# One stage for all value projections, and weights that are split again for each block, in a two-layer trunk kernel

## The chip, the cores and the metric

The kernel runs on one core of a Trainium2 chip. The metric is device time in microseconds of one launch. A core has TensorE (PE, matrix products and transposes), VectorE (DVE), ScalarE (ACT), GpSimd (POOL) and SyncE (SP), which here issues every DMA. Each engine works through a queue of its own in order, and semaphores order the engines against each other.

## The reference

x is 2048 rows of 1024 in fp32. Layer A is a gated mixer, layer B band attention with 16 heads of 64, where a chunk of 64 rows sees itself and the 8 chunks before it:

```
x = x + gmlp(rms_norm(x, g_a), ...)             # layer A
k, v = split(rms_norm(x, g_kv) @ w_kv)          # shared keys and values
q, z = split(rms_norm(x, g_b) @ w_qz)           # layer B
p = softmax(q / 8 @ k.T + rel_bias[clip(rel)])  # 64 rows against 576
x = x + ((p @ v) * silu(z)) @ w_out
out = rms_norm(x, g_f)
```

All weights are inputs, read in fp32. The keys' and values' gain g_kv and the layer's gain g_b multiply the rows of the weights, so both projections share one normalized x.

## The kernel before, in words

**Products.** Every operand of a product is split into a high part (rounded to fp32r by a cast on ACT) and a low part (what is left, a subtraction on DVE). One fp32 product is three matmuls, high x high, high x low and low x high (mm3, L115 to L118).

**Layer A** (0 to about 1347 us) leaves its result in DRAM as x1d, four blocks of 512 rows. Near its end three weights of pair 0 are scaled by POOL and stored (k_scale), and the sums of value weights that Strassen's scheme needs are stored as vwf, 7 phases x 2 halves of 128x1024.

**Layer B** goes over four time blocks t (512 rows each) and in each over 8 pairs p of heads. For a pair it projects Q, K and gate Z (24 matmuls of 128x512 each; one calls weights), then for 8 units u: score (scores, reduction with bias on DVE, exp on ACT, scaling on POOL), flip (five transposes on PE, cast on ACT, subtraction on DVE) and value (probabilities times V). ahead(t, p) is a generator that yields after each group of three matmuls; the loop at the end takes its steps between the units, so that projection of the next pair fills PE while softmax goes on.

**Values.** All values of a block come from one Strassen product (strassen, 7 phases x 2 tiles x 12 = 168 matmuls; order PHS = 1, 7, 2, 6, 5, 4, 3). For block 0 it runs during the first two scores; for block t+1 it is part of ahead(t, 7), together with normalizing x of the next block (b1: load of x1d, square on ACT, scaling on DVE, 32 transposes, copies). v_left makes the sums of x on POOL and splits them (split_s, L1106, L1107). Values go to DRAM (vhd) and are read back per pair. The **output projection** of a block is the same kind of product (o_all); its 56 steps of three matmuls are dealt out over the pairs of the next block by SHARE. Its left input, the gated output, goes through DRAM (ogd, stored at L1350), and its weights come from ows, whose sums o_sums makes during pairs 1 to 4 of t=0.

**Weights.** weights(t, p, c): at t=0 the raw weight is loaded (512 KB; pair 0 from wk0, already scaled), scaled by POOL (L163), split on ACT and DVE (L173, L174), and both halves are stored (L176, 1 MB); at t=1 to 3 the two halves are loaded ready made (kept_w, L182, 1 MB). Value weights are treated in the same way (vws). All of them live in tag T of the pool sh, 8 slots of 128x1024; tag raw has 4 slots.

**Order.** The framework lays out each engine's queue when the kernel is compiled and adds the semaphore waits; a DMA that waits on SP holds up all DMAs behind it.

Of the kernel before, what the change touches and what calls it, by code (L numbers as in the profile page):

```python
# [17 lines left out]
P = 128  # L18
# [15 lines left out]
def trunk_kernel(  # L34
# [25 lines left out]
    wk0 = [dram.tile([P, 1024], F32, name=f"wk0_{c}") for c in range(3)]  # L60
    wks = [
        [dram.tile([P, 2, 1024], F32, name=f"wks{p}_{c}") for c in range(3)] for p in range(NPAIR)
# [3 lines left out]
    }  # L66
    vws = {
        (ph, q): dram.tile([P, 2, 1024], F32, name=f"vws{ph}_{q}")
        for ph in range(1, 8) for q in range(2)
# [9 lines left out]
    vhd = [dram.tile([P, NPAIR, TB, 256], F32, name=f"vhd{t}") for t in range(NT)]  # L79
    ogd = [dram.tile([P, 2, NPAIR, 2, P], F32, name=f"ogd{t}") for t in range(NT)]  # L80
# [40 lines left out]
    xf = {}  # L121

# [4 lines left out]
    def b1(t, banks, junk):  # L127
# [4 lines left out]
        def norm(b):  # L132
            xt = sh.tile([P, D], F32, tag="raw", name=f"bx_b{t}_{b}", bufs=4)
            nc.sync.dma_start(xt[:], x1d[t][b * P : (b + 1) * P, :])
            r = sm.tile([P, 1], F32, tag="rr", name=f"rr_b{t}_{b}", bufs=4)
            nc.scalar.activation(
                junk(f"jk_b{t}_{b}"), xt[:], AF.Square, scale=1.0 / 32, accum_out=r[:]
            )
            root(r[:])
            nc.vector.tensor_scalar(xt[:], xt[:], r[:], None, op0=ALU.mult)  # L140
            xf[t, b] = xt

        def block(b):
            xt = xf[t, b]
            half = [banks(f"tr_b{t}_{b}_{h}") for h in range(2)]
            for k in range(KD):
                tpose(half[k // 4][:, k % 4, :], xt[:, k * P : (k + 1) * P], ident[:])
            x3 = xt[:].rearrange("p (k c) -> p k c", k=KD)
            for h in range(2):
                ks = slice(h * 4, h * 4 + 4)  # L150
                oh = th[:, ks, b * P : (b + 1) * P]
                ol = tl[:, ks, b * P : (b + 1) * P]
                nc.scalar.copy(oh, half[h])
                nc.scalar.copy(x3[:, ks, :], half[h])
                nc.vector.tensor_tensor(ol, half[h], oh.bitcast(F32), op=ALU.subtract)  # L155

        xT[t] = [(th[:, k, :], tl[:, k, :]) for k in range(KD)]
        return norm, block
# [6 lines left out]
    def gain_of(c):  # L165
        return (bg if c else kg)[:, :, :]

# [3 lines left out]
    def split_w(raw, name, keep):  # L171
        wh, wl = w_tile(f"wh_{name}"), w_tile(f"wl_{name}")
        nc.scalar.copy(wh[:], raw[:])  # L173
        nc.vector.tensor_tensor(wl[:], raw[:], wh[:].bitcast(F32), op=ALU.subtract)  # L174
        for i, w in enumerate((wh, wl)):
            nc.sync.dma_start(keep[:, i, :], w[:].bitcast(F32))  # L176
        return wh, wl

    def kept_w(keep, name):
        out = [w_tile(f"w{i}_{name}") for i in "hl"]  # L180
        for i, w in enumerate(out):
            nc.sync.dma_start(w[:].bitcast(F32), keep[:, i, :])  # L182
        return out
# [12 lines left out]
    def v_right(t):  # L196
        def right(ph):
            out = []
            for q in range(2):
                name = f"bv{t}_{ph}_{q}"  # L200
                if t:
                    out.append(kept_w(vws[ph, q], name))
                    continue
                raw = sh.tile([P, 1024], F32, tag="T", name=f"raw_{name}", bufs=8)
                nc.sync.dma_start(raw[:], vwf[ph, q][:])
                out.append(split_w(raw, name, vws[ph, q]))
            return out
        return right

    def o_right(t):  # L210
        def right(ph):
            return [kept_w(ows[ph, q], f"bo{t}_{ph}_{q}") for q in range(2)]
        return right

    with ExitStack() as actx:
# [698 lines left out]
        def k_scale(c):  # L914
            raw = sh.tile([P, 1024], F32, tag="raw", name=f"rk_{c}", bufs=4)
            nc.sync.dma_start(raw[:], w_kqz[0, :, c, :])
            scaled(raw, gain_of(c))
            later(2, lambda: paced(nc.sync.dma_start(wk0[c][:], raw[:])))

        for c in range(3):  # L920
            at(nin + 26 + 2 * c, lambda c=c: k_scale(c))

# [39 lines left out]
        blocks = []  # L962
        pt4x = ExitStack()

        def b_open():
            pt4 = pt4x.enter_context(tc.tile_pool(name="pt4", bufs=1, space=PSUM))
            blocks.append(b1(
                0, lambda n: pt4.tile([P, 4, P], F32, tag="t4", name=n, bufs=4)[:],
                lambda n: acc_tile(n)[:].bitcast(BF16),
            ))  # L970
            for b in range(2):
                blocks[0][0](b)

        def block0(b):
            blocks[0][1](b)
            if b < 2:
                blocks[0][0](b + 2)
# [17 lines left out]
        block0(3)  # L995
        pt4x.close()
        ptr.open(name="ptr", bufs=1, space=PSUM)
        px.close()


    with ExitStack() as bctx:
# [11 lines left out]

        sub, add = ALU.subtract, ALU.add
        tv, tg = nc.vector.tensor_tensor, nc.gpsimd.tensor_tensor
# [66 lines left out]

        PHS = (1, 7, 2, 6, 5, 4, 3)

        def strassen(name, right, left, evict):

            for ph in PHS:
                rt = right(ph)
                lt = left(ph)
                for jp in range(2):  # L1090
                    views = lt(jp)
                    ps = pmm.tile([P, 512], F32, tag="mm", name=f"{name}_{ph}_{jp}")
                    for k in range(4):
                        hi, lo = rt[k // 2]
                        c = slice((k % 2) * 512, (k % 2) * 512 + 512)
                        mm3(ps[:], *views[k], hi[:, c], lo[:, c], k == 0, k == 3)
                        if k < 3:
                            yield
                    evict(ph, jp, ps[:])
                    yield  # L1100

        def split_s(name, src):
            hi, lo = (
                sb.tile([P, 4, P], F32R, tag="S", name=f"S{i}{name}", bufs=6) for i in "hl"
            )
            nc.scalar.copy(hi[:], src)  # L1106
            tv(lo[:], src, hi[:].bitcast(F32), op=sub)  # L1107
            return [(hi[:, k, :], lo[:, k, :]) for k in range(4)]

        def v_left(t):  # L1110
            def quad(r, h):
                def of(jp):
                    c = slice((2 * jp + r) * P, (2 * jp + r + 1) * P)
                    return [(a[:, c], b[:, c]) for a, b in xT[t][4 * h : 4 * h + 4]]
                return of

            def raw(jp, r, h):
                return xf[t, 2 * jp + r][:, h * 512 : h * 512 + 512]

            def summed(ph, r, h):  # L1120
                def of(jp):
                    return split_s(
                        f"v{t}_{ph}_{jp}", raw(jp, r, h).rearrange("p (k c) -> p k c", k=4)
                    )
                return of

            def left(ph):
                if ph == 1:
                    for jp in range(2):
                        a11, a12, a21, a22 = (raw(jp, r, h) for r in range(2) for h in range(2))  # L1130
                        tg(a22, a21, a22, op=add)
                        tg(a21, a11, a21, op=sub)
                        tg(a11, a22, a11, op=sub)
                        tg(a12, a12, a11, op=sub)
                return {
                    1: quad(0, 0), 2: quad(0, 1), 4: quad(1, 1), 5: summed(5, 1, 1),
                    7: summed(7, 1, 0), 6: summed(6, 0, 0), 3: summed(3, 0, 1),
                }[ph]
            return left

        def v_evict(t):
            xa, ya = {}, {}

# [41 lines left out]
        def v_all(t):  # L1185
            yield from strassen(f"vp{t}", v_right(t), v_left(t), v_evict(t))
# [446 lines left out]
```

## Time and profile before

| | |
|---|---|
| median of 3 runs | 2928.61 us (2919.07 to 2932.9) |
| profiled execution | 2926.53 us |
| its span | 2924.7 us |
| granted TensorE clock, mean | 0.96 |
| DMA | 834.13 MB, mean 285 GB/s |
| HBM read / written | 619.20 / 201.85 MB |
| layer A | 0 to about 1347 us |
| layer B, t=0 | to about 1795 us (first score at 1369) |
| t=1, 2, 3 | to about 2161, 2521, 2816 us |
| rest of the output projection | to the end |

The span is the time from the first to the last instruction of the profiled execution. A line of the waits view names the engine that sat idle, the tile and line it was about to work on, the engine and line (or DMA) whose end released it, and then the total, the number of times and the longest. A line of the groups view gives the line, engine, operation, tiles, shapes and count, then busy time and mean duration of one, then idle time just before. Line numbers are those of the kernel before.

### The profile page before, as it was taken

Reading aid. Unit: us, or ns where it says so; the run is one execution under the profiler, and the core shown is the slowest. Engines: PE = TensorE matmul, PEld = TensorE weight load, DVE = VectorE, ACT = ScalarE, POOL = GpSimd, SP = SyncE. Lnnn points to the kernel's source line nnn. Section 1 sums busy time; section 2 is a strip of 40 time slices with the busy share of each in tenths; the row PEclk is TensorE's granted clock in tenths of the full one; section 3 lists DMA queues with packets and bytes.
Section 4 is the critical chain, followed back from the end, with each engine's and each line's share of the span. In section 5 each row is a group of like instructions: output and inputs, shape, how many; then the busy total and the mean of one; then the engine's idle time right before and its main releaser. Section 6 shows DMA issues by size and latency. Waiting matters only on the chain. (4 is left out here: it accounts for less than half of the span.)

```text
span 2924.7 us, 38938 instructions
## 1 busy us (share of the span) xinstructions
PE 2698.2 (92%) x13216; PEld 2237.6 (77%) x13216; DVE 1845.4 (63%) x3009; ACT 1246.8 (43%) x2274; POOL 888.1 (30%) x903
## 2 busy tenths in 40 slices
PE   9999999999999999998587689999899998999975
PEld 7788888888888888886365577788777887788854
DVE  5665776666776686774355465566765667566653
ACT  5332333434344343334244354455544555455532
POOL 4513153332514131232214343133322224122223
PEclk9999999999999999999787799999999999999987
DMA  8898989899888786885787788878888788986685
GB/s 304 319 326 329 377 323 326 319 344 328 316 287 306 269 337 208 287 315 196 261 287 247 247 298 288 284 244 274 284 297 293 240 277 281 301 258 215 219 291 208
DMA packets 302356, 834.13 MB, mean 285 GB/s; under 512 B 32592, under 2 KB 65360, under 8 KB 302160
## 3 DMA queue, kind: packets, MB, share of 16 engines
q1 hardware_dynamic: 302160, 831.67, 82.0%
q8 instruction: 105, 1.72, 0.2%
q14 instruction: 91, 0.75, 0.1%
HBM read 619.20 MB, written 201.85 MB: 281 GB/s over the span
## 5 line engine op out<-in xcount | busy, mean ns | idle before, releaser
L116 PE MATMUL P<-T,S 128*128 128x512 f32 x1248 | 495.2, 397 | 2.1 <-ACT S L265 2.1
L118 PE MATMUL P<-T,S 128*128 128x512 f32 x1248 | 489.4, 392 | 0.0
L117 PE MATMUL P<-T,S 128*128 128x512 f32 x1248 | 488.2, 391 | 0.6 <-DVE T L268 0.6
L1273 POOL TENSOR_SCALAR pr<-pr,sl 128x640 f32<-128x640 f32 (+4 forms) x256 | 199.2, 779 | 638.3 <-DVE sl L1272 593.9
L116 PE MATMUL pj<-hh_b,wh_b 128*128 128x512 f32 x768 | 317.9, 414 | 33.2 <-ACT wh_b L173 27.4
L118 PE MATMUL pj<-hh_b,wl_b 128*128 128x512 f32 x768 | 309.5, 403 | 12.9 <-DMA wl_b<-wks 12.5
L117 PE MATMUL pj<-hl_b,wh_b 128*128 128x512 f32 x768 | 308.7, 402 | 0.9 <-DVE hl_b L155 0.9
L1269 ACT ACTIVATE pr<-pr,nm 128x640 f32<-128x640 f32 (+4 forms) x256 | 195.3, 763 | 260.6 <-DVE nm L1262 254.9
L118 PEld LDWEIGHTS P<-T,S 128*128 128x128 f32 x1248 | 234.7, 188 | 50.2
L116 PEld LDWEIGHTS P<-T,S 128*128 128x128 f32 x1248 | 235.2, 188 | 47.0 <-ACT S L265 2.3
L117 PEld LDWEIGHTS P<-T,S 128*128 128x128 f32 x1248 | 235.2, 188 | 46.4 <-DVE T L268 1.0
L1297 DVE TENSOR_TENSOR pt<-tp,pt 128x640 fp32r<-128x640 f32 (+4 forms) x256 | 189.1, 739 | 115.4 <-ACT pt L1296 113.9
L1262 DVE CUSTOM_DVE_ANT_0 pr<-s,bias 128x640 f32<-128x640 f32 (+4 forms) x256 | 188.4, 736 | 44.7 <-PE s L1254 36.3
L116 PEld LDWEIGHTS pj<-hh_b,wh_b 128*128 128x128 f32 x768 | 149.8, 195 | 58.2 <-ACT wh_b L173 29.6
L118 PEld LDWEIGHTS pj<-hh_b,wl_b 128*128 128x128 f32 x768 | 148.6, 193 | 53.5 <-DMA wl_b<-wks 18.8
L1296 ACT CAST pt<-tp 128x640 fp32r<-128x640 f32 (+4 forms) x256 | 158.7, 620 | 64.6 <-PE tp L1293 60.8
L1293 PE MATMUL tp<-ident,pr 128*128 128x128 f32 x1120 | 168.2, 276 | 18.3 <-DVE pt L1297 13.9
L1293 PEld LDWEIGHTS tp<-ident,pr 128*128 128x128 f32 x1120 | 135.7, 141 | 57.0 <-issue 18.8
L117 PEld LDWEIGHTS pj<-hl_b,wh_b 128*128 128x128 f32 x768 | 149.3, 194 | 21.8 <-DVE hl_b L155 1.2
L1254 PE MATMUL s<-K,Qh 128*128 128x320 f32 (+1 forms) x448 | 118.3, 333 | 38.6 <-DVE nm L1262 29.2
L1321 PE MATMUL pv<-pt,V 128*128 128x256 f32 x960 | 144.9, 293 | 0.0
L1254 PEld LDWEIGHTS s<-K,Qh 128*128 128x128 f32 x448 | 84.3, 193 | 66.9 <-DVE nm L1262 39.0
(269 smaller groups left out, 5821.4 us busy)
## 6 DMA issues: line engine op xcount, KB each, us to landing
S<-hsd SPq DMA_DIRECT2D x288, 512.0 KB, 5.4
rw<-in_w_a SPq DMA_DIRECT2D x108, 512.0 KB, 6.2
A<-ytd SPq DMA_DIRECT2D x72, 512.0 KB, 5.9
wh_b<-wks SPq DMA_DIRECT2D x72, 512.0 KB, 6.2
wl_b<-wks SPq DMA_DIRECT2D x72, 512.0 KB, 6.5
hsd<-S SPq DMA_DIRECT2D x56, 512.0 KB, 4.4
V<-vhd SPq DMA_DIRECT2D x56, 512.0 KB, 4.8
wh_bo<-ows SPq DMA_DIRECT2D x56, 512.0 KB, 4.9
```

The source lines that it names most:

```text
L116: mm(ps, lh, rh, start=first, stop=False)
L117: mm(ps, lh, rl, start=False, stop=False)
L118: mm(ps, ll, rh, start=False, stop=last)
L1254: mm(ps[:, sg, :w], q[:, qb * P : (qb + 1) * P], kx[:, koff + sg * w : koff + (sg + 1) * w], start=i == 0, stop=i == 1,)
L1262: nc.vector.tensor_tensor_reduce(out=pr[:, c0:].rearrange("p (a b) -> p a b", a=nseg), in0=ps[:, :nseg, :w], in1=bias[:, c0:].rearrange("p ...
L1269: nc.scalar.activation(pr[:, c0:], pr[:, c0:], AF.Exp, scale=-1.0, bias=nm[:], accum_out=sl[:])
L1273: nc.gpsimd.tensor_scalar(pr[:, c0:], pr[:, c0:], sl[:], 1.0, op0=ALU.mult, op1=ALU.mult)
L1293: tpose(tp[:, b, :], pr[:, b * P : (b + 1) * P], ident[:])
L1296: nc.scalar.copy(oh, tp[:, b0:5, :])
L1297: nc.vector.tensor_tensor(pt[:, 1, b0 + qq : 5 + qq, cs], tp[:, b0:5, :], oh.bitcast(F32), op=ALU.subtract)
L1321: mm(po[:, 0, :], keys(i), pt[:, j, i, :], start=(t == 0 and j == 0 and i == blocks[0]), stop=(j == 1 and i == blocks[-1]),)
```

## The change

1. A **value stage** between the layers, in a pool of its own (vp). It loads each raw value weight once, splits it once and keeps the halves on chip: phases 1, 7, 5, 4, 3 in 20 tiles of the pool, phases 2 and 6 in the 8 slots of T. It makes the values of all four blocks in turn. While block t is worked on, x of block t+1 is loaded and normalized, and its 32 transposes stand at steps 20, 28, 36 and 44. For t >= 1 the transposed x goes to DRAM (xtd); pair 7 of block t-1 loads it again and splits it (reload). vws is gone, and b1 and v_all leave ahead.
2. **K, Q and gate weights**: at t=0 the raw weight is loaded, scaled, stored scaled (wk3, 0.5 MB) and split; at t >= 1 the raw weight is loaded (0.5 MB) and split again. Raw, high and low part all sit in T. k_scale leaves layer A.
3. **strassen looks one tile ahead**: after the second of a tile's four steps it asks for the next tile's weights and left input. o_left loads and sums earlier. For the last block the weights of phases 2 and 3 come raw and are split.
4. **Steps**: SHARE is (2, 7, 7, 7, 7, 7, 7, 12) in each block; the last block's output projection stands wholly behind the last pair; ahead(0, 0) begins during the first two scores.

The diff, cut to its core:

```diff
     def weights(t, p, c):
         name = f"b{t}_{p}_{c}"
+        raw = t_tile(f"raw_{name}")
+        w = w_tile(f"wh_{name}"), w_tile(f"wl_{name}")
         if t:
-            return kept_w(wks[p][c], name)
-        tag, n = ("raw", 4) if p else ("T", 8)
-        raw = sh.tile([P, 1024], F32, tag=tag, name=f"raw_{name}", bufs=n)
-        nc.sync.dma_start(raw[:], w_kqz[p, :, c, :] if p else wk0[c][:])
-        if p:
-            scaled(raw, gain_of(c))
-        return split_w(raw, name, wks[p][c])
+            nc.sync.dma_start(raw[:], wk3[p][c][:])
+        else:
+            nc.sync.dma_start(raw[:], w_kqz[p, :, c, :])
+            scaled(raw, (bg if c else kg)[:, :, :])
+            nc.sync.dma_start(wk3[p][c][:], raw[:])
+        split_in(raw, *w)
+        return w
...
+    def reload(t):
+        th, tl = x_tiles(t)
+        for b in range(TB):
+            xt = sh.tile([P, D], F32, tag="raw", name=f"xr_b{t}_{b}", bufs=4)
+            nc.sync.dma_start(xt[:], xtd[t][b][:])
...
+            nc.scalar.copy(oh, x3)
+            tv(tl[:, :, b * P : (b + 1) * P], x3, oh.bitcast(F32), op=sub)
...
     def strassen(name, right, left, evict):
...
+        ready(0)
+        for i, (ph, jp) in enumerate(todo):
...
                 mm3(ps[:], *vs[k], hi[:, c], lo[:, c], k == 0, k == 3)
+                if k == 1:
+                    ready(i + 1)
...
+    with ExitStack() as vctx:
+        vp = vctx.enter_context(tc.tile_pool(name="vp", bufs=1, reuse_waits="tile"))
+        vw = {
+            (ph, q): [vp.tile([P, 1024], F32R, name=f"vw{i}{ph}_{q}") for i in "hl"]
+            for ph in (1, 7, 5, 4, 3) for q in range(2)
+        }
+        def v_right(t):
+            def right(ph):
+                if t == 0:
+                    for q in range(2):
+                        if ph in (2, 6):
+                            vw[ph, q] = [w_tile(f"vw{i}{ph}_{q}") for i in "hl"]
+                        raw = vp.tile([P, 1024], F32, tag="st", name=f"st{ph}_{q}", bufs=2)
+                        nc.sync.dma_start(raw[:], vwf[ph, q][:])
+                        split_in(raw, *vw[ph, q])
+                return [vw[ph, q] for q in range(2)]
+            return right
...
+        for t in range(NT):
+            if t + 1 < NT:
+                for b in range(TB):
+                    norm(t + 1, b, v_junk)
+            for i, _ in enumerate(strassen(f"vp{t}", v_right(t), v_left(t), v_evict(t))):
+                if t + 1 < NT and i in (20, 28, 36, 44):
+                    block(t + 1, (i - 20) // 8)
...
-        SHARE = {1: (0, 9, 9, 9, 9, 10, 10, 0), 2: (0, 9, 9, 9, 9, 10, 10, 0)}
-        SHARE[3] = (0, 3, 4, 4, 4, 4, 4, 33)
+        SHARE = (2, 7, 7, 7, 7, 7, 7, 12)
...
-            elif t + 1 < NT:
-                norm, block = b1(t + 1, bank4, junk)
-                for b in range(TB):
-                    norm(b)
-                for b in range(TB):
-                    block(b)
-                    yield
-                yield from project(t + 1, 0)
-                yield from v_all(t + 1)
-                values(t + 1, 0)
-            if t:
-                yield from some(outs[t - 1], SHARE[t][p])
-            if t + 1 == NT and p + 1 == NPAIR:
-                yield from some(outs[t], 16)
+                if t:
+                    yield from some(outs[t - 1], SHARE[p])
+            else:
+                if t + 1 < NT:
+                    reload(t + 1)
+                if t:
+                    yield from some(outs[t - 1], 4)
+                if t + 1 < NT:
+                    yield from project(t + 1, 0)
+                    values(t + 1, 0)
+                if t:
+                    yield from some(outs[t - 1], 8)
```

More of the change, by code (lines that the diff above doesn't have):

```diff
@@ L79, in trunk_kernel @@
     vhd = [dram.tile([P, NPAIR, TB, 256], F32, name=f"vhd{t}") for t in range(NT)]
+    xtd = [[dram.tile([P, D], F32, name=f"xtd{t}_{b}") for b in range(TB)] for t in range(NT)]
     ogd = [dram.tile([P, 2, NPAIR, 2, P], F32, name=f"ogd{t}") for t in range(NT)]
@@ L121, in trunk_kernel @@
     xf = {}
+    banks = []
+    pt4x = ExitStack()
+    place = [lambda t, b: sh.tile([P, D], F32, tag="raw", name=f"bx_b{t}_{b}", bufs=4)]
+    sub, add = ALU.subtract, ALU.add
+    tv, tg = nc.vector.tensor_tensor, nc.gpsimd.tensor_tensor
     def root(r):
@@ L199, in right @@
             for q in range(2):
-                name = f"bv{t}_{ph}_{q}"
-                if t:
[L202 to L206, printed above, removed]
-            return out
-        return right
[L210 to L213, printed above, removed]
+                name = f"bo{t}_{ph}_{q}"
@@ L1102, in split_s @@
[L1102 to L1139, printed above, removed]
@@ L1533, in trunk_kernel @@
         run(gen)
-        gen = v_all(0)
+        values(0, 0)
+        first = ahead(0, 0)
         for u in range(2):
             score(0, 0, u)
-            take(gen, 8)
-        run(gen)
-        values(0, 0)
+            take(first, 4)
         before = None
```

319 lines of the change are left out of this document (168 added, 151 removed).

## The prediction

> **What bounds the kernel now.** I read the busy shares and the 40 slices of the page first, then stretches of the span by stage, then in each stage the waits of TensorE (PE), then single lines.
>
> ```profile
> span 2924.7 us, 38938 instructions
> PE 2698.2 (92%) x13216; PEld 2237.6 (77%) x13216; DVE 1845.4 (63%) x3009; ACT 1246.8 (43%) x2274; POOL 888.1 (30%) x903
> PE   9999999999999999998587689999899998999975
> PEclk9999999999999999999787799999999999999987
> ```
>
> PE is the bound in nearly every slice. The exceptions are slices 19 to 23 (1390 to 1750 us: layer B's block t=0) and the last two, and there the granted clock falls too. A gain can come from these holes or from work taken off PE. This change takes no matmul away, so only holes count.
>
> Next, stretches; columns are the window, its length, each engine's busy time (PE first, with its instructions), granted clock, DMA share, GB/s.
>
> ```profile
> 1060.00:1320.00 260.00, 260.00 (x1149) 215.29 (x1148) 184.74 (x215) 91.61 (x141) 67.68 (x42) 1.00 0.78 283
> 1347.00:1369.00 22.00, 15.81 (x61) 11.08 (x60) 11.89 (x12) 8.23 (x14) 6.68 (x10) 0.92 0.75 256
> 1369.00:1481.00 112.00, 69.13 (x189) 44.75 (x189) 41.77 (x74) 34.26 (x61) 20.37 (x21) 0.75 0.77 271
> 1532.00:1574.00 42.00, 32.52 (x134) 26.09 (x132) 23.93 (x52) 19.35 (x44) 19.93 (x24) 0.80 0.75 258
> 1574.00:1625.00 51.00, 34.65 (x137) 26.16 (x136) 23.44 (x55) 19.73 (x45) 17.19 (x23) 0.80 0.73 247
> 1625.00:1672.00 47.00, 33.58 (x129) 25.98 (x129) 22.63 (x51) 18.90 (x43) 17.47 (x23) 0.75 0.72 238
> 1672.00:1710.00 38.00, 31.31 (x138) 24.66 (x137) 19.11 (x46) 16.08 (x37) 14.07 (x19) 0.78 0.83 277
> 1710.00:1737.00 27.00, 25.50 (x137) 20.66 (x136) 19.73 (x48) 15.71 (x39) 11.65 (x20) 1.00 0.82 278
> 1737.00:1795.00 58.00, 50.94 (x252) 41.78 (x252) 31.74 (x72) 31.62 (x71) 21.54 (x30) 0.97 0.85 290
> 1795.00:2087.00 292.00, 275.02 (x1519) 233.25 (x1518) 184.07 (x372) 144.44 (x275) 77.11 (x105) 0.99 0.84 278
> 2087.00:2161.00 74.00, 63.65 (x325) 54.02 (x324) 50.67 (x93) 38.97 (x77) 27.82 (x29) 0.93 0.85 285
> 2446.00:2521.00 75.00, 65.31 (x332) 54.85 (x332) 51.52 (x93) 39.22 (x79) 28.07 (x30) 0.95 0.88 292
> 2816.00:2925.00 109.00, 60.91 (x220) 46.42 (x218) 41.18 (x71) 21.91 (x46) 30.27 (x27) 0.74 0.70 240
> ```
>
> The first row is a stretch of layer A with nothing but 128x512 matmuls at full clock: 260/1149 = 0.226 us each. For the others I count as **lost** the length less busy time times clock. The value projections of block 0 (1369:1481) lose 112 - 69.13x0.75 = 60 us. Pairs 2 to 5 of t=0 (the four rows 1532 to 1710) lose 16, 23, 22 and 14, together 75; pair 6 (1710:1737), with as many instructions, loses 1.5. Pair 7 of t=0, 1, 2, which carries the next block's value projections, loses 8.6, 14.8 and 13. The tail loses 109 - 60.91x0.74 = 64.
>
> **The change part by part.** One: the value projections of block 0. What holds them now:
>
> ```profile
> DVE wl_bv L174 <- ACT wh_bv L173: 48.0, 11, 8.6
> ACT wh_bv L173 <- DMA raw_bv<-vwf: 46.2, 7, 8.3
> PE vp L116 <- ACT wh_bv L173: 35.2, 12, 4.7
> SPq L176 <- ACT wh_bv L173: 35.0, 10, 5.9
> L173 ACT CAST wh_bv<-raw_bv x13: 1029/1044/1045, 1375.3 to 1475.2; 128x1024 fp32r<-128x1024 f32 x13
> L174 DVE TENSOR_TENSOR wl_bv<-raw_bv,wh_bv x13: 1220/1224/1993, 1376.6 to 1476.3; 128x1024 fp32r<-128x1024 f32 x13
> raw_bv<-vwf SPq DMA_DIRECT2D x13, 512.0 KB, 4.6
> ```
>
> It is a ring: PE waits for the split, the split for the raw load, and the load is queued on SP behind the store of the halves (L176), which waits for the split before. Thirteen casts from 1375.3 to 1475.2 make 99.9/12 = 8.3 us per half of a phase; 14 halves give the 112 us. The change drops both stores, gives raw data two buffers of their own (st), and holds the halves in place. A buffer then turns in load 4.6 + cast 1.04 + subtraction 1.22 + some 0.6 for issue and semaphores = 7.5 us, and two buffers serve one phase of two halves: 7 x 7.5 = 52 us. PE needs 168 x 0.226 = 38. From below it can't be under 38; from above the old pace gives 112. I take 52, the sum of the rows. The two scores that share the old window, some 4 us, move to later: **-56**. Ahead of it the transposes of block 1 and its four loads of x now stand in front of the first value matmul, and SP has those loads before the first raw weight: I take 11 us lost at the start, against 22 - 15.81x0.92 = 7 now: **+4** (0 to +15).
>
> Two: blocks 1 to 3 move from pair 7 of t=0, 1, 2 into the new stage. Each is 168 matmuls (38 us) and 32 transposes; the work goes along unchanged. In the new stage a block needs no weight traffic; ACT and DVE split halves of x and evict, as in pair 7 now, where DVE is busy 50.67 us of 74, so I take 4 us lost per block (0 to 10), mainly at the seams: +12. Where they leave, these waits go:
>
> ```profile
> PE pj L118 <- DMA wl_b<-wks: 11.4, 12, 2.3
> PE tr_b L147 <- DVE hl_b L155: 8.6, 4, 3.2
> PE pj L116 <- DMA wh_b<-wks: 5.5, 5, 2.0
> PE vp L117 <- DMA wl_bv<-vws: 4.7, 6, 1.3
> PE vp L116 <- DMA wh_bv<-vws: 3.6, 4, 1.4
> ```
>
> (PE alone, 1795 to 2521.) The rows tr_b and vp are pair 7's; they hold 17 of the 28 us that its t=1 and 2 lose. What comes in their place is four reloads of transposed x with a split (ACT, DVE) each, early in pair 7, and projection of the next block must wait for the last. I leave 5 us lost per pair 7, so -4, -10 and -8, about -23: **-11** together.
>
> Three: pairs 1 to 5 of t=0. Stores shrink from 1 MB of halves, after the split, to 0.5 MB of scaled raw data that waits for POOL alone; and in the order of instructions the gate weight's load now stands ahead of the store of K.
>
> ```profile
> PE pj L116 <- ACT wh_b L173: 23.7, 8, 4.7
> ACT wh_b L173 <- POOL raw_b L163: 22.5, 13, 3.3
> SPq L176 <- ACT wh_b L173: 37.5, 11, 6.3
> SPq L1062 <- DVE K L1058: 9.7, 4, 4.7
> raw_b<-in_w_kqz SPq DMA_DIRECT2D x17, 512.0 KB, 5.5
> L163 POOL TENSOR_TENSOR raw_b<-raw_b,bg x11: 1891/1896/2347, 1533.4 to 1721.0; 128x1024 f32<-128x1024 f32 x11
> ```
>
> (1495 to 1737.) The same ring, with POOL's 1.9 us in it. SP still has each next load behind a store, now behind POOL instead of the split (2.3 us shorter), and the gate weight skips the whole wait for K. Of three weights I give 2 us each for the split and 2 for K's store, 8 us per pair, over four pairs: **-32** of the 75 lost. From below it is 0, if the output-weight sums of these pairs (o_sums, unchanged) hold SP as before; at most -70, were they to run like pair 6.
>
> Four: at t=1 to 3 each of 72 weights comes as 0.5 MB raw and is split again. ACT gets 72 x 1.04 = 75 us more and DVE 72 x 1.22 = 88; both are under 70% busy there, DVE 184 of 292, so neither becomes the bound by sum. What counts is latency. Raw, high and low part take 3 of the 8 slots T, o's phase holds 4; so in the order of instructions the low part of two weights in three waits for the last matmul of the weight before, on DVE, with this weight's first two matmuls, five transposes and some value matmuls in PE's order between. DVE's queue behind it holds the flips' subtractions and the score reductions, for which PE waits next. A pair takes 292/7 = 42 us, 14 per weight, against load 5.5 + cast 1.04 + subtraction 1.22 = 8, so the load itself is hidden. What is exposed is bounded by pair 6 from below:
>
> ```profile
> L174 DVE TENSOR_TENSOR wl_b<-raw_b,wh_b 128x1024 fp32r<-128x1024 f32 x3 | 3.7, 1225 | 1.9 <-ACT wh_b L173 1.9
> L173 ACT CAST wh_b<-raw_b 128x1024 fp32r<-128x1024 f32 x3 | 3.1, 1043 | 0.7 <-POOL raw_b L163 0.7
> ```
>
> There three weights are split on chip and the pair loses 1.5 us, 0.5 each. From above all of cast, subtraction and 0.6 of semaphores shows, 2.9 each. I take pair 6's 0.5, for two of three weights: 48 x 0.5 = +24 (0 to +205). Half the weight bytes lets the loads land earlier: of the waits for wl_b and wh_b (17 us) I take 12 as gone. Net **+12**.
>
> A page speaks against this step. The Trainium skill, "SBUF — State Buffer", section "Who interferes with whom", says that a DVE instruction with two SBUF inputs contends with a GpSimd instruction that reads SBUF, and that the loser waits for the whole instruction. POOL is busy 77.11 of 292 us here; if a split in four met the 0.78 us of a POOL instruction (the next row), that would be 72 x 0.26 x 0.78 = 15 us of DVE time, and the sum would be 2825.
>
> ```profile
> L1273 POOL TENSOR_SCALAR pr<-pr,sl 128x640 f32<-128x640 f32 (+4 forms) x256 | 199.2, 779 | 638.3 <-DVE sl L1272 593.9
> ```
>
> The trace agrees in kind: of the 13 subtractions above the median is 1.22 us and the longest 1.99.
>
> Five: the tail.
>
> ```profile
> PE bo L116 <- ACT Sho L1106: 28.5, 3, 12.4
> ACT Sho L1106 <- DMA A<-ogd: 21.0, 2, 11.0
> ```
>
> (2815 to 2925.) Now a third of the last block's output projection stands in pair 7 and the rest stops three times for its left input, which makes a round trip through DRAM from the last pair's values. After the change all 56 steps stand behind pair 7: the last value product comes early, and phases 1 and 7 (11 us), which need only the first heads, cover the round trip; the look one tile ahead puts loads and splits a tile earlier. Then weights bound it: 2 MB per phase, at the 290 GB/s of the best row above 7 us for 5.4 us of matmuls, and 1 MB for phases 2 and 3, which come raw. I leave 5 of the 28.5 us of waits; the clock, 0.74 now, comes back to about 0.9, worth 60.91 x 0.2 = 12: **-35** (0 to -50). The even shares of the output projection in other pairs, and the key scaling that leaves layer A (three loads and stores under a full PE), I take at 0: PE is the bound there; if one of them uncovered a load, a wait of about 2 us like those above.
>
> **Sum:** +4 - 56 - 11 - 32 + 12 - 35 = -118. The profiled execution took 2926.5 us; the median of the three is 2928.6, 2 above. So **2810 us**, a saving of 4%.
>
> **Rivals.** R1, splits exposed (slower): at t=1 to 3 DVE stands at the low part until PE is done, the flips behind it come late, and each of 72 weights costs 2.9 us: +209 instead of +24, giving 2995. It turns the change into a loss from (118 + 24)/72 = 2.0 us per weight. For it speaks the wait for PE ahead of DVE's queue; against it pair 6, 0.5 per weight, though there the slots don't wait for PE.
>
> R2, the value stage keeps the old pace for block 0 (loads with xo, x and xtd traffic in front): 8.3 us a half, +60, 2870. R3, the pairs of t=0 don't change, because o_sums hold SP and not the stores: +32, 2842; this and a tail that is bound by its loads as before are how the change doesn't do what it says; with both, 2877. R4, all covers hold: t=0 like pair 6 (-38), no exposure of splits (-24): 2748.
>
> **How the numbers follow.** Forecast, 2775 to 2840: 0.53. R2, R3 or both, 2840 to 2900: 0.20. R4, under 2775: 0.13. R1: 0.14, of which 0.10 above 2943, where each split costs over 2 us, and 0.04 about no change. A measurement of this kernel can tell 0.5% (15 us). Faster by more: 0.86; within: 0.04; slower: 0.10. Range 2750 to 2900: it leaves out R1 (0.14) and the lower half of R4 (0.06).
>
> **What would show it.** In the profile after: value matmuls of four blocks in one stretch of about 200 us from 1362, block 0 in about 52, with granted clock above 0.9; pairs 2 to 5 of t=0 about 35 us each; PE waits on the split of wh_b and wl_b at t=1 to 3 below 40 us in all; no waits over 8 us for Sho in the tail. I am wrong if DVE's queue wait for PE at the split comes back as PE waiting for nm, pt or K, if block 0 takes 80 us or more, or if the first output phases still stop for A.

## The result, and the profile after

The changed kernel takes 2816.61 us (median of 4 runs, 2814.59 to 2819.17) against 2929.16 us before (4 runs): a ratio of 0.9621, 95% interval 0.9596 to 0.9647. The forecast was 2810. The profiled execution took 2819.17 us, its span 2817.4.

The head of the page of after, as it was shown of before:

```profile
span 2817.4 us, 38771 instructions
PE 2673.3 (95%) x13216; PEld 2220.0 (79%) x13216; DVE 1955.1 (69%) x3091; ACT 1322.6 (47%) x2356; POOL 907.6 (32%) x903
PE   8999999999999999999799878999989999999997
PEclk9999999999999999999999898999999999999997
DMA packets 274421, 732.42 MB, mean 260 GB/s; under 512 B 29488, under 2 KB 62256, under 8 KB 274224
```

PE has the same 13216 matmuls, 25 us less busy time (less of it at a low clock) and 82 us less idle time. DVE has 110 us more to do and ACT 76, mostly the second split; traffic falls by 102 MB. The long hole from 1390 to 1750 us is gone from the slices of PE: what is left of it are one slice from 1338 to 1409 us (the start of the value stage) and three from 1550 to 1761 us (pairs 0 to 5 of t=0).

The same stretches as before the change, in the windows view of after (window, length, PE and the other engines' busy time, granted clock, DMA share, GB/s):

```profile
1347.00:1365.00 18.00, 7.05 (x38) 6.47 (x35) 9.24 (x15) 11.61 (x21) 10.53 (x10) 0.62 0.57 219
1365.00:1413.00 48.00, 42.85 (x175) 31.03 (x174) 32.42 (x48) 28.96 (x48) 4.75 (x5) 1.00 0.79 267
1413.00:1540.00 127.00, 124.16 (x575) 101.94 (x574) 92.37 (x140) 62.33 (x128) 53.38 (x39) 1.00 0.55 188
1540.00:1581.00 41.00, 35.47 (x162) 29.10 (x161) 19.13 (x48) 18.16 (x39) 12.09 (x21) 0.92 0.80 257
1581.00:1612.00 31.00, 26.31 (x128) 21.12 (x126) 21.43 (x52) 17.50 (x43) 16.22 (x22) 0.89 0.76 237
1612.00:1648.00 36.00, 28.74 (x132) 22.85 (x132) 24.81 (x53) 18.84 (x44) 18.80 (x23) 0.91 0.79 269
1648.00:1691.00 43.00, 30.22 (x132) 22.93 (x132) 24.71 (x54) 19.45 (x45) 19.89 (x24) 0.88 0.77 258
1691.00:1730.00 39.00, 30.32 (x134) 23.38 (x134) 23.61 (x52) 19.35 (x43) 17.58 (x22) 0.87 0.76 250
1730.00:1767.00 37.00, 32.44 (x148) 25.16 (x148) 20.18 (x49) 17.38 (x39) 15.95 (x22) 0.91 0.75 247
1794.00:1822.00 28.00, 23.91 (x109) 18.95 (x108) 23.09 (x48) 19.48 (x41) 11.31 (x18) 0.82 0.61 193
2086.00:2129.00 43.00, 37.21 (x199) 31.00 (x198) 35.98 (x64) 25.28 (x46) 14.02 (x17) 0.92 0.79 268
2400.00:2445.00 45.00, 39.67 (x204) 32.95 (x203) 36.05 (x65) 25.51 (x46) 14.96 (x18) 0.89 0.79 267
1365.00:1822.00 457.00, 400.65 (x1825) 317.86 (x1824) 300.38 (x582) 236.62 (x500) 179.11 (x211) 0.94 0.70 232
1822.00:2739.00 917.00, 872.40 (x4851) 740.54 (x4850) 692.39 (x1285) 531.03 (x959) 262.79 (x348) 0.98 0.65 211
2739.00:2817.00 78.00, 55.62 (x214) 42.08 (x213) 48.75 (x72) 25.91 (x51) 32.61 (x26) 0.82 0.71 246
```

Row 2 is the value product of block 0: 48 us where it took 112, and nearly all of it busy. Row 3 holds blocks 1 to 3, 2.8 us of PE's idle time in 127. Rows 4 and 5 run from there to the start of pair 2 of t=0, rows 6 to 9 are pairs 2 to 5, rows 10 to 12 pair 7 of t=0, 1 and 2. The last three rows cut layer B in three: value stage and t=0, then t=1 to 3, then what follows the last score (the tail). They are what the experiments are compared by, since the work in each is nearly the same in all of them (the matmul count stands in brackets). Their bounds are the starts of the first value product, of the first score of t=1 and of the last score, rounded.

Before the change the stretch up to pair 2 of t=0 that followed the value product of block 0 was

```profile
1481.00:1532.00 51.00, 46.47 (x223) 38.00 (x222) 30.31 (x64) 23.26 (x54) 11.03 (x19) 0.96 0.80 275
```

The waits of PE in after, first one from 1347 to 1365, then from 1822 to 2739, then in the tail:

```profile
PE tr_b L154 <- DVE rr_b L125: 10.9, 1, 10.9
```

```profile
PE tp L1319 <- DVE pt L1323: 16.1, 19, 2.5
PE pj L114 <- DVE wl_b L191: 11.2, 20, 1.2
PE pj L112 <- ACT wh_b L190: 8.1, 7, 1.8
PE s L1280 <- DVE nm L1288: 6.9, 5, 3.1
```

```profile
PE bo L113 <- DMA wl_bo<-ows: 3.5, 1, 3.5
PE bo L113 <- DVE wl_bo L191: 3.4, 2, 3.1
PE bo L112 <- ACT Sho L257: 1.2, 1, 1.2
```

The loads of ready halves are no longer waited for; the split is, 19 us over 68 recorded weights. In the tail 1.2 us of the 28.5 for the left input are left.

### The profile page after: what moved, and what is told of

Same layout as the page of the kernel before. It is cut to its first block, busy times and chain, and to the rows that moved or that the text cites. A ratio compares the mean times of both kernels' runs of the same rounds, so it can differ in the third digit from the quotient of the medians.

```text
span 2817.4 us, 38771 instructions
## 1 busy us (share of the span) xinstructions
PE 2673.3 (95%) x13216; PEld 2220.0 (79%) x13216; DVE 1955.1 (69%) x3091; ACT 1322.6 (47%) x2356; POOL 907.6 (32%) x903
## 5 line engine op out<-in xcount | busy, mean ns | idle before, releaser
L1299 POOL TENSOR_SCALAR pr<-pr,sl 128x640 f32<-128x640 f32 (+4 forms) x256 | 206.1, 806 | 603.0 <-DVE sl L1298 529.8
L114 PE MATMUL pj<-hh_b,wl_b 128*128 128x512 f32 x768 | 312.6, 407 | 14.2 <-DVE wl_b L191 13.9
L191 DVE TENSOR_TENSOR wl_b<-raw_b,wh_b 128x1024 fp32r<-128x1024 f32 x96 | 130.7, 1361 | 46.1 <-ACT wh_b L190 40.1
L1347 PE MATMUL pv<-pt,V 128*128 128x256 f32 x960 | 152.2, 294 | 2.0 <-ACT pt L1322 2.0
L190 ACT CAST wh_b<-raw_b 128x1024 fp32r<-128x1024 f32 x96 | 100.7, 1049 | 111.1 <-DMA raw_b<-wk 57.6
```

The source lines that it names most:

```text
L114: mm(ps, ll, rh, start=False, stop=last)
L191: tv(wl[:], raw[:], wh[:].bitcast(F32), op=sub)
L1299: nc.gpsimd.tensor_scalar(pr[:, c0:], pr[:, c0:], sl[:], 1.0, op0=ALU.mult, op1=ALU.mult)
L1347: mm(po[:, 0, :], keys(i), pt[:, j, i, :], start=(t == 0 and j == 0 and i == blocks[0]), stop=(j == 1 and i == blocks[-1]),)
```

## The experiments

All ratios are to the kernel before, on the same chip in the same group of runs, with their 95% interval: x1 to x4, x5 to x8 and x9 to x12 are a group each. The kernel before took 2929 us beside after and 2937 to 2941 in these groups, so a ratio of one group stands against one of another to about 0.4%, 12 us; what is smaller is read from the stages. Their lengths come from one profile each. The first stage moved between 457 and 466 us among kernels that do the same there, so only more than that counts. The last score is issued well before the last units end, so all 168 matmuls of the last block's output projection stand in the tail of every kernel; what differs is how many of block 2's stand there too. After, x1, x4 and x5 have 175 matmuls of output projection in the tail, x2 183 and x3 188, and about as many fewer at t=1 to 3; at 0.226 us each that is 2 us for x2 and 3 for x3.

| kernel | ratio (interval) | value stage and t=0 | t=1 to 3 | tail |
|---|---|---|---|---|
| after | 0.9621 (0.9596 to 0.9647) | 457 | 917 | 78 |
| x1 halves kept | 0.9761 (0.9739 to 0.9782) | 509 | 909 | 81 |
| x2 value stage alone | 0.9742 (0.9720 to 0.9764) | 509 | 885 | 103 |
| x3 old shares | 0.9591 (0.9565 to 0.9617) | 466 | 889 | 98 |
| x4 no look ahead | 0.9548 (0.9528 to 0.9568) | 466 | 887 | 82 |
| x5 left input alone ahead | 0.9562 (0.9547 to 0.9576) | 466 | 889 | 85 |
| x6 ahead at the ends only | 0.9517 (0.9495 to 0.9539) | 460 | 891 | 79 |
| x7 split twice | 0.9687 (0.9671 to 0.9703) | 464 | 941 | 77 |
| x8 sums late | 0.9524 (0.9499 to 0.9548) | 436 | 921 | 78 |
| x9 x6 and x8 together | 0.9439 (0.9423 to 0.9454) | 435 | 892 | 77 |
| x10 x9, more cover in pair 7 | 0.9447 (0.9427 to 0.9467) | 437 | 896 | 79 |
| x11 x9, store on ACT | 0.9433 (0.9413 to 0.9454) | 438 | 882 | 75 |
| x12 after, store on ACT | 0.9504 (0.9489 to 0.9519) | 438 | 904 | 79 |

### Undoing the parts

**x1** puts K, Q and gate weights back to stored halves:

```diff
         if t:
-            nc.sync.dma_start(raw[:], wk3[p][c][:])
+            for i in range(2):
+                nc.sync.dma_start(w[i][:].bitcast(F32), wks[p][c][:, i, :])
+            return w
...
-            nc.sync.dma_start(wk3[p][c][:], raw[:])
         split_in(raw, *w)
+        for i in range(2):
+            nc.sync.dma_start(wks[p][c][:, i, :], w[i][:].bitcast(F32))
```

> The changed kernel, but K, Q and gate weights are treated as before: at t=0 both halves are stored after the split (1 MB), at t=1 to 3 both halves are loaded ready made and nothing is split again. Theory (three holes filled; the second split is nearly free): pairs 2 to 5 of t=0 lose 75 us again instead of 46 (+29), and at t=1 to 3 the waits on the split (19 us) are replaced by waits for loads (about 18): 2816 + 29 = 2845, 2835 to 2855. Rival A (less traffic is what made layer B faster everywhere): t=1 to 3 get slower too, by 40 us or more: over 2885. Rival B (the second split is exposed and costs): t=1 to 3 get faster by 30 or more: 2815 or less.

It measured 2867.34 us, 1.4 points of ratio (41 us) above after. The windows of x1, its first stage and t=1 to 3:

```profile
1368.00:1877.00 509.00, 418.07 (x1827) 330.24 (x1825) 287.34 (x575) 231.52 (x492) 173.06 (x209) 0.89 0.71 236
1877.00:2786.00 909.00, 862.50 (x4848) 738.62 (x4847) 619.43 (x1219) 466.91 (x895) 254.18 (x350) 0.98 0.79 252
```

All of the cost is in t=0, 509 us against 457 to 466. At t=1 to 3 the kernel without a second split is 8 us shorter (909 against 917) though its data rate is 20% higher (252 GB/s against 211). So neither rival holds: less traffic makes nothing clearly faster at t=1 to 3, and the split of 72 weights costs some 8 us there, 0.1 each, less than the 13 us by which this stage moved in x12 below without an edit to it. The theory had the place right and the size too small: 29 us expected at t=0, 43 to 52 found. A part of that may be x1's own: its raw weight keeps a slot of T, where the kernel before took it from the tag raw; this was not tried apart.

**x2** is x1 without the look one tile ahead and with the old shares, so little more than the value stage alone (the last block's raw weights of phases 2 and 3, the earlier o_left and the early ahead(0, 0) stay in it):

```diff
-        ready(0)
         for i, (ph, jp) in enumerate(todo):
+            ready(i)
...
-                if k == 1:
-                    ready(i + 1)
...
-        SHARE = (2, 7, 7, 7, 7, 7, 7, 12)
+        SHARE = {1: (0, 9, 9, 9, 9, 10, 10, 0), 2: (0, 9, 9, 9, 9, 10, 10, 0)}
+        SHARE[3] = (0, 3, 4, 4, 4, 4, 4, 33)
...
+                if t + 1 == NT:
+                    yield from some(outs[t], 16)
```

> The value stage alone: weights as before (both halves stored and loaded), no look one tile ahead, shares of the output projection as before with 16 steps of the last block in pair 7. Theory: only the value hole is filled, 112 to 48 us for block 0 and some 10 us of pair 7's losses: 2929 - 70 = 2859 plus up to 5 for pair 7's reload, 2850 to 2875. Rival A (the gain is one thing, relief of the DMA queues, and comes with the weights): 2890 or more. Rival C (look ahead and shares matter little, the tail is bound by weights): the same as the run with halves, 2845.

2861.39 us, as the theory had it. The windows of x2 at t=1 to 3 and in the tail:

```profile
1874.00:2759.00 885.00, 853.00 (x4843) 734.23 (x4842) 608.96 (x1217) 474.46 (x896) 250.03 (x349) 0.99 0.79 253
2759.00:2862.00 103.00, 58.10 (x221) 43.84 (x219) 47.12 (x75) 25.91 (x50) 30.37 (x27) 0.77 0.68 234
```

The stage, with those small parts, is worth 2.6%, two thirds of the whole gain. Beside x1 the tail is the news. Look ahead and new shares save 22 us in the tail (103 to 81) and lose 24 at t=1 to 3 (885 to 909); 2 us of each are matmuls that stand elsewhere. The ratios of x1 and x2 can't be told apart: parts 3 and 4 of the change gained in the tail and gave it back earlier.

**x3** takes after and puts the old shares back, with 12 steps of the last block's product in pair 7 (the diff is x2's without its first part, and with 12 in place of 16).

> The changed kernel with the old shares of the output projection, and 12 steps of the last block's in pair 7 (the look one tile ahead stays, so 12 and not 16: a load of the left input would come too early otherwise). Theory: the tail was shortened because all 56 steps stand behind the last value product, so that the first 24 cover the round trip of the gated output; with 12 of them spent before it, 6 us of cover are left of 12, and 6 to 20 us come back: 2825 to 2837. Rival C (tail bound by weights, or made good by the look ahead): within 4 us of 2816.

0.9591: no worse than after, where the theory expected 6 to 20 us more. The windows of x3, the output projection's matmuls in the tails of after and of x3 (the windows view of tile bo), and PE's waits in x3's tail:

```profile
1835.00:2724.00 889.00, 853.33 (x4832) 727.11 (x4833) 677.11 (x1277) 534.52 (x956) 253.21 (x344) 1.00 0.67 211
2724.00:2822.00 98.00, 61.62 (x227) 45.66 (x225) 48.16 (x78) 27.36 (x53) 34.42 (x30) 0.84 0.71 253
```

```profile
2739.00:2817.00 78.00, 51.21 (x175) 37.83 (x175) 8.67 (x13) 2.35 (x4) 0.82 0.71 246
2724.00:2822.00 98.00, 57.22 (x188) 40.46 (x186) 10.04 (x15) 2.34 (x4) 0.84 0.71 253
```

```profile
PE bo L112 <- DMA wh_bo<-ows: 8.8, 2, 5.4
PE bo L113 <- DMA wl_bo<-ows: 6.1, 1, 6.1
PE bo L112 <- ACT Sho L257: 5.8, 3, 4.3
```

The tail is 20 us longer, of which 13 matmuls more are 3 us, and it stops for its weights (15 us against 3.5) and its left input (5.8 against 1.2) again. But t=1 to 3 take 28 us less, 25 with those 13 matmuls put back, although the look ahead still stands there. So the step on the tail holds, with the loads of weights as the larger part, and t=1 to 3 of after pay for something in parts 3 and 4.

**x4** takes after and drops the look ahead everywhere (the first part of x2's diff):

> The changed kernel; the Strassen products ask for weights and left input of a tile only when the tile starts. In the value stage block 0's loads and splits then start a tile later: with two buffers for raw weights the ring of 7.5 us per phase is no longer beside the matmuls of the phase before but partly behind them. Theory: value stage +10 to +30, splits of left inputs exposed by about 1.9 us (cast 0.62, subtraction 0.69, semaphores) in up to 14 tiles of 8 products where the scheduler doesn't move them ahead by itself, tail +5: 2835 to 2870. Rival (the framework's scheduler and the free slots move loads ahead anyway): within 6 us of 2816.

It is faster than after, 0.9548, where the theory expected 20 to 50 us more. The windows of x4:

```profile
1833.00:2720.00 887.00, 856.24 (x4844) 733.79 (x4844) 692.36 (x1282) 528.09 (x959) 261.23 (x348) 0.99 0.69 217
2720.00:2802.00 82.00, 56.90 (x217) 43.57 (x215) 47.98 (x73) 26.22 (x52) 32.40 (x26) 0.79 0.68 240
```

The theory fell. The value stage didn't need the look ahead (first stage 466, as in x3, which has it), the tail is only 4 us longer, so the shares and not the look ahead shortened it; and at t=1 to 3, beside the new shares, the look ahead costs 30 us (917 against 887, same work and same shares). Against x2, which splits nothing at t=1 to 3 (885, or 887 with its 8 matmuls put back), 887 leaves nothing for the second split and the new shares together. With x3 that makes four corners, each with its matmuls put back: 887 and 892 with the old shares (x2 without the look ahead and the split, x3 with both), 887 with the new shares and no look ahead, 917 with both. So neither the look ahead nor the even shares cost much by themselves; the 25 to 30 us come only where both stand.

### What the look ahead costs

Two candidates: the next tile's weights (on chip earlier, so more of the 8 slots T are held by the output projection), or the next tile's left input (its splits stand on ACT and DVE ahead of scores and flips). **x5** asks ahead for the left input alone:

```diff
-                if jp == 0:
-                    rts[ph] = right(ph)
                 views[i] = left(ph, jp)
...
         for i, (ph, jp) in enumerate(todo):
+            if jp == 0:
+                rts[ph] = right(ph)
```

> The look ahead brought 29 us of lost time to t=1 to 3 in the changed kernel (92 lost; 64 without it). Here only the left input of the next tile is asked for ahead, its weights when the tile starts. Theory (weights asked for early take 4 more of the 8 slots T, from the pairs' weights): t=1 to 3 lose as without the look ahead, about 64, 0.955 of the kernel before. Rival (the left input's splits, put ahead on ACT and DVE, delay flips and scores): the cost stays, 0.962.

0.9562, and 889 us at t=1 to 3. The cost goes with the weights, not with the splits. (The expectation's 92 and 64 us are counted against a floor that no line here shows; by the windows after loses 62 us there and x4 39.) **x6** keeps the look ahead in the value stage and the last output projection:

```diff
+        look = name[:2] == "vp" or name == f"bo{NT - 1}"
+        if look:
+            ready(0)
         for i, (ph, jp) in enumerate(todo):
+            if not look:
+                ready(i)
```

> Look ahead kept in the value stage and in the last block's output projection only, where no pair's weights compete. Theory: t=1 to 3 as without it (64 us lost), tail 4 us shorter (34 against 38), value stage 1 shorter: 0.9535 of the kernel before, about 2798 where that is 2935. Rival (run-to-run spread explains the 13 us between the kernels with and without): 0.962.

0.9517; the expectation was 0.9535. The windows of x5 (t=1 to 3) and of x6 (t=1 to 3, tail):

```profile
1834.00:2723.00 889.00, 856.00 (x4847) 734.37 (x4848) 690.89 (x1283) 528.62 (x959) 262.47 (x348) 0.99 0.69 217
```

```profile
1825.00:2716.00 891.00, 858.35 (x4849) 734.64 (x4848) 692.45 (x1285) 528.66 (x959) 263.21 (x348) 0.99 0.69 216
2716.00:2795.00 79.00, 53.60 (x215) 39.68 (x213) 47.41 (x72) 25.77 (x51) 32.18 (x26) 0.88 0.71 250
```

Six kernels with the even shares but without early weights beside a pair (x4, x5, x6, x9, x10, x11) have 882 to 896 us at t=1 to 3; those with both (after, x8, x12) have 904 to 921. That the slots T are the means by which early weights do harm agrees with this, but it was not tried by itself, and it can't be all: SP's wait at the load of output weights (L219) for the projections that hold the slots is 108.7 us in after and 78.2 in x4, but 109.6 in x3, which doesn't pay for it. Why the old shares bear the early loads stays open.

### What the second split costs

**x7** makes the low part twice at t=1 to 3:

```diff
         split_in(raw, *w)
+        if t:
+            tv(w[1][:], raw[:], w[0][:].bitcast(F32), op=sub)
```

> The changed kernel with the subtraction for the low part made twice at t=1 to 3 (the second writes the same values): 72 x 1.22 = 88 us more on DVE, each in front of the first use of the low part. Theory (the split is mostly hidden, PE's waits for it were 11 us in 20 of 68): half or less shows, +20 to +45: 2845 to 2870 where the changed kernel takes 2825. Rival R1 (every split stands in PE's way): +88 or more. Rival (wholly hidden): within 8 us.

0.9687, 0.0066 above after: 19 us of 2941, give or take the 12 between groups. The windows of x7, then its two subtractions in the groups view, then PE's wait for them:

```profile
1832.00:2773.00 941.00, 881.66 (x4843) 743.50 (x4844) 760.44 (x1351) 530.96 (x960) 285.02 (x349) 0.97 0.65 205
```

```profile
L191 DVE TENSOR_TENSOR wl_b<-raw_b,wh_b 128x1024 fp32r<-128x1024 f32 x68 | 88.3, 1298 | 28.7 <-PE pj L113 18.1 <-ACT wh_b L190 10.3
L205 DVE TENSOR_TENSOR wl_b<-raw_b,wh_b 128x1024 fp32r<-128x1024 f32 x68 | 85.3, 1254 | 0.3
```

```profile
PE pj L114 <- DVE wl_b L205: 22.6, 24, 3.4
```

Of 85 us and more put on DVE, ahead of the first use, 24 show at t=1 to 3 (941 against 917). Rival R1, by which each split is fully exposed, is out; "wholly hidden" is out too. One subtraction more costs about 0.3 us per weight (24 us for 72), near the 0.5 that pair 6 gave for a whole split.

### What still holds t=0

**x8** moves the output-weight sums from pairs 1 to 4 to pairs 4 to 7, **x12** sends the store of the scaled weight through ACT's queue, so that SP's next load doesn't stand behind it:

```diff
-                if t == 0 and 1 <= p <= 4:
-                    todo = o_sums(p - 1)
+                if t == 0 and p >= 4:
+                    todo = o_sums(p - 4)
```

```diff
-            nc.sync.dma_start(wk3[p][c][:], raw[:])
+            nc.scalar.dma_start(wk3[p][c][:], raw[:])
```

> The changed kernel with the output-weight sums (o_sums) at pairs 4 to 7 of t=0 in place of 1 to 4. Pairs 2 to 5 still lose 56 us by floor (46 by the windows). Rival R3 (o_sums hold SP and are what is left of the loss): pairs 1 to 3 run like pair 6 now, 2 to 4 us lost each, and pairs 5 to 7 lose 10 to 20 each instead. Theory (the ring of load, POOL, split and store is what holds, o_sums beside it only lengthen the queue): pairs 1 to 3 still lose 6 or more each. The total within 15 us of 2825 in both.

> The changed kernel with only that store moved to ACT's queue. With the sums at pairs 1 to 4 SP is full of their loads and stores. Theory (the sums hold the pairs, as their move showed, and not the store): within 8 us of the changed kernel, 0.960 to 0.964. Rival (the ring over the store holds): pairs 2 to 5 lose 20 us less, 0.955.

The windows of x8: the first stage, and pairs 1 to 3 (1581 to 1671):

```profile
1366.00:1802.00 436.00, 390.18 (x1828) 314.31 (x1826) 297.04 (x579) 235.15 (x496) 179.38 (x211) 0.96 0.72 235
1581.00:1610.00 29.00, 26.18 (x133) 21.75 (x133) 22.44 (x49) 18.13 (x43) 18.02 (x24) 0.94 0.85 269
1610.00:1637.00 27.00, 25.56 (x137) 20.98 (x136) 19.93 (x49) 16.54 (x39) 11.60 (x19) 1.00 0.83 264
1637.00:1671.00 34.00, 27.95 (x137) 22.11 (x136) 22.82 (x51) 18.44 (x43) 20.65 (x24) 0.95 0.77 247
```

and of x12 the first stage:

```profile
1366.00:1804.00 438.00, 395.14 (x1832) 314.40 (x1833) 300.29 (x584) 236.68 (x503) 179.52 (x211) 0.96 0.73 242
```

and what SP waited for at that store (L202) in after, from 1581 to 1767:

```profile
SPq L202 <- POOL raw_b L181: 18.0, 8, 5.0
```

Without the sums pair 2 takes 27 us with 1.4 lost, the pace of pair 6, with the store still in SP's queue. Pair 1 loses 4.4 and pair 3 7.4, where all three lose 34 in after: the ring by itself holds little, and the theory that it does fell for two of three pairs. Pairs 5 to 7, which the rival had lose 10 to 20 us each, lose 7, 5.5 and 13, and the total is 2800 us, not within 15 of 2825. With the sums in place and the store off SP the stage is as short, 438 us: the theory that only the sums hold fell too. Both kernels save about 20 us in the first stage. **x9** is x6 and x8 together, **x11** adds x12's store to it:

> The two edits that paid, together: look ahead only in the value stage and the last output projection, and the output-weight sums at pairs 4 to 7 of t=0. Alone they gave 0.9517 and 0.9524 against 0.9621. Theory (two separate places, t=1 to 3 and t=0): the savings add up, 0.942, about 2765 where the kernel before takes 2935. Rival (one thing, less pressure on the slots T and SP): 0.950.

> As the run with both edits, and at t=0 the scaled raw weight is stored from ACT's queue, so that no load waits on SP behind it. Theory (SP's order behind the store holds part of what t=0 still loses): 5 to 15 us off, 0.938. Rival (ACT, which then stands until POOL has scaled, loses as much as SP gains): within 5 us, or slower.

x9 gives 0.9439; the sum of its two parts would be 0.942, closer than the 0.4% between groups, and both stages keep their gain (435 and 892 against 457 and 917).

Once the sums are moved, the store's queue makes no difference (435 and 438 in the first stage, 0.9439 and 0.9433). I read the two as rivals for one resource: the order of SP's queue, in which a load stands behind stores that wait. Either one taken out frees what it held; some 60 us are still lost in x9's first stage (435 less 390.24 x 0.96), and what holds those was not tried. x12 also gained 13 us at t=1 to 3 and x11 10 against x9, where the edit does nothing but shift the order of the queues; why stays open.

**x10** puts ten steps of output projection, not four, ahead of the next projection in pair 7, at a faster pace (steps_of returns 37 there):

> As the run with both edits, and in pair 7 of t=1 and 2 ten steps of the output projection (not 4) stand ahead of the next block's projection, taken at a faster pace. Theory (pair 7 loses 8 to 10 us because projection waits for the last split of the reloaded x): two pairs gain 4 to 6 us each, 0.939. Rival (DVE, full there with four splits of 1.2 to 2.3 us beside the flips, is what holds): no change beyond 3 us.

0.9447, no gain. Windows of pair 7 of t=1, two of after and one of x10, show what holds:

```profile
2098.00:2104.00 6.00, 3.69 (x24) 3.04 (x22) 6.00 (x7) 3.33 (x7) 4.07 (x3) 1.00 0.85 289
2104.00:2110.00 6.00, 3.26 (x12) 2.32 (x13) 5.88 (x14) 3.38 (x7) 1.05 (x2) 0.63 0.78 281
2077.00:2083.00 6.00, 2.12 (x13) 1.47 (x12) 5.88 (x9) 1.62 (x5) 1.92 (x2) 0.89 0.80 281
```

For 12 us of after DVE (third engine column, 6.00 and 5.88 of 6) is full, with splits of reloaded x between the reductions and flips for which PE waits; in x10 it is as full (5.88) while PE is busy 2.12 of 6. More matmuls ahead don't shorten DVE's queue.

## Why the prediction was right, step by step

The sum was -118, the change measured -112.5. Loss is again length less busy time times granted clock.

- **Start of the value stage, +4:** 18 - 7.05x0.62 = 13.6 lost against 7, +6. It is a single wait of after, 10.9 us of the transposes of block 1 for its norm on DVE, as the step had it in kind.
- **Value product of block 0, -56:** 52 us forecast, 48 measured, with the clock at 1.00 in place of 0.75; the loss fell from 60 to 5. R2, the old pace of 8.3 us per half, is out. PE is busy 42.85 of the 48 us, so what is left is PE's own time more than the ring of loads.
- **Blocks 1 to 3, -11:** 4 us lost per block forecast, 2.8 in all found. But pair 7 of t=1 and 2 still loses 8.8 and 9.7, not 5: the reload was priced as a wait for its last split, and it is DVE's whole queue (x10). With pair 7 of t=0 (8.4) the losses there are 27 us and not 15: 12 worse here against 9 better in the stage. (The step's own terms, 4, 10 and 8, make 22 and not 23.) Together -7.
- **Pairs of t=0, -32:** the loss of pairs 2 to 5 fell from 75 to 46, -29; that it is the queue of SP agrees with x8 and x12. The step left out that pairs 0 and 1 now carry the same queue: 1540 to 1612 loses about 10 us more than 1481 to 1532 did, so -19 in all. R3, that o_sums hold SP, was half right: about 20 us of what is left go when either they or the store leave.
- **Second split, +24 less 12:** x1 gives +8, x4 against x2 nothing, both within the scatter of the stage; x7 shows 0.3 us per added subtraction. R1 is out, though DVE's queue is felt where the text said it would be: PE's waits for the flips (tp for pt) are 16.1 us against 5.5 before, while those for nm fell from 13.9 to 6.9. Outside pair 7 of t=1 and 2 the loss at t=1 to 3 (by the same windows view) went from 45 to 40 us, -5 where +12 was forecast, with the cost of the look ahead in it.
- **Tail, -35:** the loss fell from 64 to 32, -32, and the new shares did it (x3: the tail is 20 us longer with a part of the steps spent ahead; x4: without look ahead only 4). Its two terms came out otherwise: the waits for the left input fell by 27 us, from 28.5 to 1.2, and the clock came back to 0.82 and not 0.9, so that PE's busy time fell by 5 us and not 12. Weights bound what is left less than thought: 3.5 us of PE's waits for loads.
- **What failed:** "the look one tile ahead puts loads and splits a tile earlier" was counted as a gain of the tail alone, and the even shares were taken at 0. At t=1 to 3 the two together cost 25 to 30 us (x3 to x6), which no term held. The text had four slots T held by the output projection; with the look ahead it asks for more. That the sum came out right all the same is in part luck: the pairs of t=0 fell 13 us short, pair 7 with the stage 4, the tail and the rest 6, and t=1 to 3 made up 17, because the second split cost next to nothing; without the look ahead those blocks would have been about 30 us shorter still. R4 (2748) was not reached by the change; the lowest found is 2768 (x11), with the look ahead kept to the ends, the sums late and the store on ACT.

## What to carry to other kernels

Work that is bound by a ring of load, split and store is worth collecting in one stage with buffers of its own, because the ring is paid once and the clock comes back with it (0.75 to 1.00 here). Looking ahead can cost time even where it adds no work: here it was worth 4 us in the tail, where no pair's weights compete, and cost up to 30 beside the pairs, so it belongs only where nothing competes. When two causes meet in one place, as the sums and the store in one queue or the look ahead and the even shares, taking out either looks like the whole cure, so test them together before counting both.

## What the runs showed of the hardware

The subtractions of a split have two lengths. Of after, all of layer B, then the group at t=1 to 3 with its mean:

```profile
L191 DVE TENSOR_TENSOR wl_b<-raw_b,wh_b x96: 1205/1225/2310, 1521.9 to 2701.9; 128x1024 fp32r<-128x1024 f32 x96
L191 DVE TENSOR_TENSOR wl_b<-raw_b,wh_b 128x1024 fp32r<-128x1024 f32 x68 | 92.1, 1354 | 10.0 <-PE pj L113 4.9 <-ACT wh_b L190 4.2
```

Of all 114 recorded subtractions of L191, 71 ran with POOL idle and took 1.22 us, none of them over 1.4; of the 43 that met a POOL instruction, 18 took over 1.4 and the mean was 1.59. That is 43 x 0.37 = 16 us of DVE time. The Trainium skill ("SBUF — State Buffer", "Who interferes with whom") says that such an instruction of DVE, with two SBUF inputs, contends with a GpSimd instruction that reads SBUF; the trace agrees, with 18 of 43. The prediction worked out 15 us of DVE time for the 72 weights of t=1 to 3; their 68 recorded subtractions took 1354 ns in the mean, 68 x (1354 - 1222) = 9 us over the short length. In the kernel's time it shows little, since x7 put 85 us on DVE for 19 us.
